# A chunked RWKV-7 recurrence on one core: outputs with both heads of a pair side by side, turned by four full transposes a chunk; keys turned by eight

## The chip, the cores and the metric

The kernel is one launch on one core of a Trainium2 chip. The core has five engines with a queue each, which run their instructions in order: TensorE (PE in the rows; its weight loads are PEld), VectorE (DVE), ScalarE (ACT), GpSimd (POOL) and SyncE (SP), which issues the DMAs. The metric is the device time of the launch in microseconds (us); the number compared is the median of several runs.

## The reference, cut to what matters

The program is one step of a two-layer encoder over 1024 prompt tokens and 64 sample tokens, with 1024 features in 16 heads of 64. Layer 0 mixes time by a recurrence per head over the tokens, and then has a feed-forward part; layer 1 has windowed attention and a second feed-forward part. The change is in the recurrence:

```
def step(s, inp):                       # s [head, value, key]
    r_t, w_t, k_t, v_t, a_t, b_t = inp
    sa = einsum('bhvk,bhk->bhv', s, a_t)
    s = s * w_t[:, :, None, :] + sa[..., None] * b_t[:, :, None, :] + v_t[..., None] * k_t[:, :, None, :]
    return s, einsum('bhvk,bhk->bhv', s, r_t)
...
s_fin, y = lax.scan(step, s0, seq_in)
yc = y - mean(y, axis=-1, keepdims=True)
yn = yc * rsqrt(mean(yc * yc, axis=-1, keepdims=True) + LNX_EPS)
yn = yn.reshape(bsz, t_len, D_MODEL) * lnx_w + lnx_b
bonus = (sum(rh * kh * r_k, axis=-1, keepdims=True) * vh).reshape(bsz, t_len, D_MODEL)
out = ((yn + bonus) * g) @ w_o
```

## The kernel before

Two kinds of work share the core. The dense products (projections, feed-forward, lines 422 to 424) take each fp32 operand as two float32r parts and sum three matmuls; their weights come by DMA, are cast on ACT (L382) and subtracted on DVE or POOL (L383). The recurrence (class `Rwkv`, tiles named `r_...`, its PSUM tiles `p_rp`, `p_rc`, `p_ry`) works in 17 chunks of 64 tokens: eight, then eight, then the sample's one. All of its products go through `mm` (L73) and `tr` (L77), so that tiles, not lines, tell them apart.

A chunk has four parts. `prep` makes the scaled keys `BK`, queries `AR` and the triangles `X` (tile `r_G`), which need no state. `prep2` inverts the triangles, mostly on DVE, and turns the keys into `BT`. `chain` is what the state `M` passes through: `U0p`, `Up`, the state's increment `Sp`, and the outputs `Y` (tile `p_ry`, one buffer), which are the sum of `AR` times the state and `X` times the stacked operand `sv`. `post` normalises `Y` over the 64 values of each head on DVE, ACT and POOL into `yc`, turns `yc` back to features on the partitions in the place of `Y`, applies the gate `g` and writes `z`.

The heads stand in pairs: head 2j on partitions 0 to 63, head 2j + 1 on 64 to 127. In `Y` of before, the partition is (head of the pair, token) and the free axis (pair, value). A full transpose of a pair's columns would mix both heads, so `post` turns each head by itself:

```
for j in range(8):
    self.tr(Y[0:64, j, :], yc[0:64, j, :], c["id"][0:64, 0:64])
    self.mm(Y[64:128, j, :], lhsT=yc[64:128, j, :], rhs=c["id"][64:128, 64:128], start=True, stop=True)
```

The order on each engine is fixed when the program is built: a scheduler emits the instruction of the lowest priority number that it holds to be ready. `recur` gives the chain and `prep2` a number ahead of the dense work, and `prep` and `post` of a chunk one behind it for all but their products, so that dense products fill PE between the recurrence's pieces. At run time the queues are fixed, and an instruction that waits holds up what stands behind it on its engine.

Of the kernel before, what the change touches and what calls it, by code (L numbers as in the profile page):

```python
# [21 lines left out]
def bc(ap, n):  # L22
    """[p, a] -> [p, a, n], each value n times"""
    return ap.unsqueeze(len(ap.shape)).broadcast_to(list(ap.shape) + [n])


def mid(ap, n):
    """[p, a] -> [p, n, a], the row n times"""
    return ap.unsqueeze(1).broadcast_to([ap.shape[0], n] + list(ap.shape[1:]))


class Two:
    """Puts the products of a stream of instructions at another priority than the rest of it."""
# [15 lines left out]
class Rwkv:  # L49
    """The chunked WKV-7 recurrence: chunks of 64 tokens, 16 heads in 8 pairs."""  # L50
# [20 lines left out]
    def mm(self, *a, **k):  # L71
        with self.two:
            self.nc.tensor.matmul(*a, **k)  # L73
# [8 lines left out]
    def start(self):  # L82
        """the part of W that stays zero"""
        nc = self.nc
        self.W = self.sb.tile([128, 8, 64], F32, name="W", tag="W", bufs=1)
        nc.gpsimd.memset(self.W, 0.0)

    def prep(self, ch):
        """all that does not need the state; heads 2j on partitions 0-63, heads 2j + 1 on 64-127"""
# [13 lines left out]
        # 1 / |kk|^2 as the lanes of inverse() hold it: [(parity, half of the tokens, 4 times, pair), token]  # L103
# [12 lines left out]
        # the products of the decays up to each token, and before it  # L116
# [10 lines left out]
        # r P  # L127
        V.tensor_tensor(out=AR[:, :, 1, :], in0=r, in1=P, op=ALU.mult)
        # k (1 + (a - 1) k_a)
# [4 lines left out]
        # kk a / P and -kk Pex without the norm of kk, whose square inverse() divides by  # L134
# [3 lines left out]
        # r k r_k  # L138
# [3 lines left out]
        # the four triangles of each head: [(b, k) of the key, (a, r) of the query]  # L142
# [10 lines left out]
        # sum(r k r_k) v  # L153
# [7 lines left out]
    def prep2(self, d):  # L161
# [4 lines left out]
        # the strict triangle of b is spent: a takes its place  # L166
# [3 lines left out]
        flat2 = lambda x: x.rearrange("p a b -> p (a b)")  # L170
        BT = d["BT"] = self.t([128, 16, 64], "BT")
        ps = [self.pp().rearrange("p (a b) -> p a b", a=8) for _ in range(2)]
        for i in range(8):
            for par in range(2):
                h = slice(64 * par, 64 * par + 64)
                self.tr(ps[par][:, i, :], flat2(d["BK"][h, i]), self.c["id"][h, h])
        for par in range(2):
            S.copy(BT[:, 8 * par:8 * par + 8, :], ps[par])

    def inverse(self, X, nl):  # L180
        """D (I - T D)^-1 of the strict triangles T, transposed, with D = 1 / |kk|^2: first the blocks of 32 by
        substitution, a lane for each block and each fourth of its rows, then the block beside them"""
        nc, c = self.nc, self.c
        V, S, G = nc.vector, nc.scalar, nc.gpsimd
        W = self.W
# [13 lines left out]
        # two columns j, j + 1 at a time: row j + 1 takes what it adds by way of column j  # L199
        one = NL.rearrange("p a b -> p (a b)")[:, 32:1024:66]  # L200
        ev = NL.rearrange("p (a two) b -> p a two b", two=2)
        # Z: rows 8 r + 4 h + (0 .. 3) in the half h, so that neither half waits for what it has just written
# [7 lines left out]
        for j in range(30, 0, -2):  # L210
            # from the first place to the last, and back
# [19 lines left out]
        for h in range(2):  # L231
            XO = Z[:, h, 1].rearrange("p a b -> p (a b)")                   # [s, (r g pair)]
            V.transpose(out=XO, in_=XL[:, h].rearrange("p a b -> p (a b)"))
# [24 lines left out]
    def chain(self, ch, d, M):  # L258
        """M [128 = (parity, key), pair, value]: the state's transpose; returns the next"""
        nc = self.nc  # L260
        V, S, G = nc.vector, nc.scalar, nc.gpsimd
        # rows of the stacked operands: the state, later U, on 0-63; the values on 64-127
# [11 lines left out]
        for i, j, h in heads:  # L274
            self.mm(Y[h, j, :], lhsT=d["AR"][h, j, 1, :], rhs=M[h, j, :], start=j == 0, stop=False)
# [8 lines left out]
        for i, j, h in heads:  # L284
            self.mm(Sp[h, j, :], lhsT=BT[:, 8 * (i % 2) + j, :], rhs=sv[:, i, :], start=True, stop=True)
        for i, j, h in heads:
            self.mm(Y[h, j, :], lhsT=X[:, 8 * (i % 2) + j, 64:128], rhs=sv[:, i, :], start=False, stop=j == 7)
# [5 lines left out]
    def post(self, ch, d, Y):  # L293
# [18 lines left out]
        # back to the features on the partitions, in the place of Y  # L312
        for j in range(8):
            self.tr(Y[0:64, j, :], yc[0:64, j, :], c["id"][0:64, 0:64])
            self.mm(Y[64:128, j, :], lhsT=yc[64:128, j, :], rhs=c["id"][64:128, 64:128], start=True, stop=True)
# [9 lines left out]
TA, TB, TBJ = 512, 576, 580          # tokens of the halves; TBJ: with the columns between the streams  # L325
SOFF = 516                           # first column of the sample stream in a TBJ wide tile
SCALE = 0.125

# columns of `vecs`: [128, 8] each, feature = 128 * column + partition
# [4 lines left out]
RING, EXTRA, EARLY = 11, 4, 13       # pairs of operand tiles; more after the recurrence, and before it  # L334
# [5 lines left out]
class Dense:  # L340
    """Products with the features on the partitions: both operands cut into two float32r parts."""
# [12 lines left out]
    def st(self, w=584):  # L354
        return self.t([128, w], "st", 4)

    def tmp(self):
        """like st(), with tiles of its own as long as there are the early ones"""
        return self.t([128, 580], "es", 4, sb=self.esb) if self.esb else self.st()
# [11 lines left out]
    def weight(self, src, rows=128, raw=None):  # L371
        """a [rows, n] block of DRAM in pieces of 512 columns, each as (hi, lo)"""
# [14 lines left out]
    def part(w, o, n):  # L387
        """columns of a weight"""
# [4 lines left out]
    def pair(self, late=False):  # L393
        """the two tiles of an operand; late: it outlives the early ones"""
# [4 lines left out]
    def free(self, *pairs):  # L399
        """the last instruction that reads them is out"""  # L400
# [6 lines left out]
    def split(self, x, rows=128, eng=None, late=False):  # L407
        """x as a pair"""
# [9 lines left out]
    def mm(self, ps, parts):  # L418
        """ps = sum of the products; parts: (w hi, w lo, x hi, x lo)"""
# [6 lines left out]
    def full(self, src, xs, groups, evac):  # L426
        """one tile of 128 outputs of a product over 8 x 128 features"""
# [6 lines left out]
    def first(self, ws, xs, groups, evac):  # L434
        """full() of three tiles of outputs, which take each operand in turn as it comes"""
# [11 lines left out]
    def low(self, src, M, tag):  # L447
        """the weights of a low-rank product, as long as there are the early tiles: for each tile of features
        the high parts of its M columns, and beside them the low ones"""
# [10 lines left out]
    def low_banks(self, tag, groups):  # L460
        """banks of the recurrence, before it starts"""
# [3 lines left out]
    def low_step(self, ps, w, k, x, groups):  # L465
        """what the tile k of the features adds; up to 64 columns take the high part of x with both of theirs"""
# [10 lines left out]
    def low_sum(self, p, M, n):  # L477
        """of the products with the two parts of the weights"""
# [5 lines left out]
    def behind(self, i, before):  # L484
        """i waits for an instruction that it does not depend on"""
# [3 lines left out]
    def stack(self, t, x, q):  # L489
        """x [n, .] into the columns q of t [2 n, .]: its two parts, one below the other"""  # L490
# [5 lines left out]
class Norm:  # L496
    """1 / rms of each token, on all partitions, from tiles that come one by one"""
# [17 lines left out]
    def finish(self):  # L515
        """in two steps, for other products to come between them"""
# [11 lines left out]
        # diagonal blocks, which a product with ones spreads over the partitions  # L528
# [13 lines left out]
def go(job, *sides):  # L542
    """emits a job, with a step of each of the sides after each of its own"""
# [8 lines left out]
def several(n, gen):  # L552
    """n steps of a generator in one"""
# [8 lines left out]
def tile_stream_step(ctx: ExitStack, tc: tile.TileContext, I, O):  # L562
# [13 lines left out]
    def load(half):  # L576
        """the input; the column before the tokens is left for the row before them"""
# [17 lines left out]
    # the table of Sqrt, before it is waited for  # L595
# [9 lines left out]
    # 1 - mu  # L605
# [9 lines left out]
    def put(name, half, j, stg):  # L615
        """the feature tile j of a half into the chunks of a scratch array"""
# [6 lines left out]
    def inputs(half, hs):  # L623
        """the normalised input with the row before it in column 0"""
# [16 lines left out]
        for j, h in enumerate(hs):  # L641
            if j in pool:
                G.tensor_tensor(out=h[:, 1:T + 1], in0=h[:, 1:T + 1], in1=rs[:, :T], op=ALU.mult)
            else:
                i = V.scalar_tensor_tensor(out=h[:, 1:T + 1], in0=h[:, 1:T + 1], scalar=vec["norm_mix0"][:, j:j + 1], in1=rs[:, :T],
                                           op0=ALU.mult, op1=ALU.mult)
                # not ahead of the first products' operands
# [26 lines left out]
    def streamed(hs, half, name, step):  # L674
        """mixes whose tiles are spent one step after they come"""
# [5 lines left out]
    def decay(half, hs):  # L681
# [10 lines left out]
        # the rows of ones take w0, whose parts are on the rows 64 and 96  # L692
# [3 lines left out]
        def summed(hh, ch, n, sg):  # L696
            """over the tokens of each chunk"""
# [33 lines left out]
    def rate(half, hs, two):  # L731
        """two: a pair, its first tile for this, the second for gate()"""
# [64 lines left out]
    def rkv(half, name, xs, ws=()):  # L797
        """ws: the weights of the first tiles of outputs, which are there already"""
# [3 lines left out]
        def tokens(j, stg):  # L802
            """the values with the tokens on the partitions"""
# [50 lines left out]
    def held(gen):  # L854
        """the tiles of a mix, each once a pair that lasts is free for it"""
# [14 lines left out]
    def mixed_in(half, get, xs, res):  # L870
        """the outputs of the recurrence, which pass through the places of the residual stream"""
# [10 lines left out]
    def mix_out(half, xs, norm):  # L882
        """w_o of the time mixing, and the residual stream"""
# [9 lines left out]
    def fresh(half, x, fast=False):  # L893
        """the next norm of a residual stream"""
# [4 lines left out]
    def normed(norm, gain, xs):  # L899
        """the residual stream, normalised with a gain"""  # L900
# [11 lines left out]
    class Ffn:  # L912
        """keep: of how many pairs of tiles the second product is left to rest()"""
# [107 lines left out]
    def recur(chunks, M, base, low):  # L1021
        """the chunks in turn, what does not need the state one chunk ahead"""
# [104 lines left out]
class Attention:  # L1127
    """Grouped-query attention over the band of three chunks, with sinks. The tile m * 4 + i of the queries
# [284 lines left out]
```

## Time and profile before

| what | value |
|---|---|
| median of 3 runs | 3094.4 us (3092.99 to 3098.16) |
| the profiled execution, first to last instruction | 3098.9 us |
| PE busy | 2948.1 us, 95% |
| DVE busy | 1905.6 us, 61% |
| ACT busy | 1371.1 us, 44% |
| POOL busy | 921.6 us, 30% |
| recurrence on PE | from about 260 to 1215 us |

The page gives one execution. Of what lies around the span the page has no figure; the span is 4.5 us above the median of the runs. Busy shares are means over the whole span, in which the recurrence takes less than a third.

### The profile page before, as it was taken

How to read it: one execution, taken by the hardware profiler on the slowest of the kernel's cores; microseconds unless marked ns; L12 is line 12 of the kernel's file. 1: busy time of each engine (PE TensorE's matmuls, PEld its weight loads, DVE VectorE, ACT ScalarE, POOL GpSimd, SP SyncE). 2: the span in 40 equal slices, each digit the busy share in tenths (PEclk: the TensorE clock that was granted, in tenths of full speed). 3: DMA queues.
4: the chain of work that ended last, by engine and by line, in shares of the span. 5: the costliest groups of instructions: out<-in, count | busy, mean ns of one | idle time of the engine just before them, and what ended most of it. 6: DMA issues, size and time to landing. Idle time of an engine off the chain costs nothing. (4 is left out here: it accounts for less than half of the span.)

```text
span 3098.9 us, 52449 instructions
## 1 busy us (share of the span) xinstructions
PE 2948.1 (95%) x20126; PEld 2520.6 (81%) x20126; DVE 1905.6 (61%) x3964; ACT 1371.1 (44%) x2489; POOL 921.6 (30%) x768
## 2 busy tenths in 40 slices
PE   6899898998899999999999999999999999999998
PEld 5677677886677777887778999888667889899998
DVE  8887788968898984356654333565555334633334
ACT  6767655434555442344553222344454233322222
POOL 6464233423333322224311222243111222322221
PEclk9998778988899999999999999999999999999999
DMA  4645443334223224332212222222122332322222
GB/s 143 171 121 152 116 123 91 106 99 143 79 83 96 86 66 127 103 112 84 70 45 69 82 82 82 76 84 82 55 65 65 96 96 75 102 83 83 85 85 69
DMA packets 262051, 289.16 MB, mean 93 GB/s; under 512 B 125028, under 2 KB 143972, under 8 KB 261800
## 3 DMA queue, kind: packets, MB, share of 16 engines
q1 hardware_dynamic: 261800, 285.81, 30.8%
q8 instruction: 158, 2.59, 0.3%
q14 instruction: 93, 0.76, 0.1%
HBM read 243.18 MB, written 41.16 MB: 92 GB/s over the span
## 5 line engine op out<-in xcount | busy, mean ns | idle before, releaser
L422 PE MATMUL dp<-xh,wh 128*128 128x288 f32 (+2 forms) x3480 | 1184.5, 342 | 26.5 <-DVE hx L951 7.0
L423 PE MATMUL dp<-xl,wh 128*128 128x288 f32 (+2 forms) x3480 | 1174.9, 338 | 9.5 <-DVE xl L415 6.9
L424 PE MATMUL dp<-xh,wl 128*128 128x288 f32 (+2 forms) x3480 | 1172.3, 337 | 0.0
L382 ACT CAST wh<-wr 128x512 fp32r<-128x512 f32 x730 | 445.8, 619 | 821.7 <-PE dp L423 635.2
L422 PEld LDWEIGHTS dp<-xh,wh 128*128 128x128 f32 x3480 | 669.2, 193 | 100.5 <-DVE hx L951 9.9
L423 PEld LDWEIGHTS dp<-xl,wh 128*128 128x128 f32 x3480 | 669.9, 193 | 72.3 <-DVE xl L415 8.8
L424 PEld LDWEIGHTS dp<-xh,wl 128*128 128x128 f32 x3480 | 670.2, 193 | 61.4 <-issue 5.6
L383 DVE TENSOR_TENSOR wl<-wr,wh 128x512 fp32r<-128x512 f32 x487 | 377.6, 779 | 444.2 <-ACT wh L382 435.5
L383 POOL TENSOR_TENSOR wl<-wr,wh 128x512 fp32r<-128x512 f32 x243 | 336.0, 1383 | 997.3 <-ACT wh L382 894.1
L422 PE MATMUL dp<-mh,wh 128*128 128x288 f32 (+1 forms) x808 | 255.0, 316 | 3.6 <-DVE hx L951 2.6
L424 PE MATMUL dp<-mh,wl 128*128 128x288 f32 (+1 forms) x808 | 254.6, 315 | 0.0
L423 PE MATMUL dp<-ml,wh 128*128 128x288 f32 (+1 forms) x808 | 253.8, 314 | 0.0
L951 DVE TENSOR_TENSOR a_xB<-dp,a_xB 128x288 f32<-128x288 f32 x352 | 158.1, 456 | 82.4 <-PE dp L424 81.9
L932 DVE TENSOR_TENSOR st<-st,dp 128x288 f32<-128x288 f32 (+1 forms) x132 | 70.0, 531 | 216.8 <-PE dp L424 216.4
L934 POOL TENSOR_TENSOR xl<-st,xh 128x288 fp32r<-128x288 f32 (+1 forms) x102 | 101.2, 993 | 334.2 <-ACT xh L933 322.1
L422 PEld LDWEIGHTS dp<-mh,wh 128*128 128x128 f32 x808 | 152.5, 189 | 13.5 <-DVE hx L951 3.8
L424 PEld LDWEIGHTS dp<-mh,wl 128*128 128x128 f32 x808 | 152.4, 189 | 8.1 <-issue 1.8
L423 PEld LDWEIGHTS dp<-ml,wh 128*128 128x128 f32 x808 | 152.6, 189 | 6.8 <-issue 0.8
L951 DVE TENSOR_TENSOR hx<-dp,hx 128x512 f32<-128x512 f32 x176 | 119.8, 685 | 48.2 <-PE dp L424 47.9
L191 ACT COPY r_f<-r_G 32x1024 f32<-32x1024 f32 x68 | 134.7, 1981 | 32.5 <-DVE r_G L152 21.2
L216 DVE TENSOR_TENSOR r_f<-r_f,r_f 128x60 f32<-128x60 f32 (+5 forms) x476 | 117.5, 278 | 0.5
L930 ACT ACTIVATE st<-dp 128x288 f32<-128x288 f32 (+1 forms) x132 | 62.2, 471 | 93.2 <-PE dp L424 92.8
(344 smaller groups left out, 4003.3 us busy)
## 6 DMA issues: line engine op xcount, KB each, us to landing
wr<-in_ffn_in SPq DMA_DIRECT2D x352, 256.0 KB
wr<-in_ffn_out SPq DMA_DIRECT2D x176, 256.0 KB
wr<-in_rkv SPq DMA_DIRECT2D x90, 256.0 KB
wr<-in_rwo SPq DMA_DIRECT2D x32, 256.0 KB
wr<-in_wq SPq DMA_DIRECT2D x32, 256.0 KB
wr<-in_wo SPq DMA_DIRECT2D x32, 256.0 KB
r_r_s<-s_s SPq DMA_DIRECT2D x17, 256.0 KB
r_sv<-s_vt SPq DMA_DIRECT2D x17, 256.0 KB
```

The source lines that it names most:

```text
L191: S.copy(st[32 * q:32 * q + 32].rearrange("p (t g j) -> p t g j", g=4, j=8), src)
L216: V.tensor_tensor(out=Z[:, h, 1:3, r0:4, 0:j], in0=Z[:, h, a, r0:4, j:j + 2].rearrange("p r c -> p c r").unsqueeze(3).broadcast_to([128, 2 ...
L382: nc.scalar.copy(h, x)
L383: (nc.gpsimd if self.turn % 3 == 0 else nc.vector).tensor_tensor(out=l, in0=x, in1=h, op=ALU.subtract)
L422: self.nc.tensor.matmul(ps, lhsT=wh, rhs=xh, start=i == 0, stop=False)
L423: self.nc.tensor.matmul(ps, lhsT=wh, rhs=xl, start=False, stop=False)
L424: self.nc.tensor.matmul(ps, lhsT=wl, rhs=xh, start=False, stop=i == last)
L930: S.activation(t[o], p, AF.Silu)
L932: V.tensor_tensor(out=t[o], in0=t[o], in1=p, op=ALU.mult)
L934: G.tensor_tensor(out=a.lo[:, q], in0=t[o], in1=a.hi[:, q], op=ALU.subtract)
L951: V.tensor_tensor(out=self.x[m][:, q], in0=p, in1=self.x[m][:, q], op=ALU.add)
```

## The change

Three things change. The remaining lines of the diff remove comments and docstrings, so that later line numbers move by up to 11.

1. `Y` gets another layout: the partition is (parity of the pair's number, token), and the free axis (pair of pairs, head of the pair, value), so both heads of a pair stand side by side in 128 columns. `post` then turns `yc` by four transposes of 128 x 128 in place of eight transposes and eight products of 64 x 64.
2. The part of `Y` from the state was 16 products in a row, of the two heads of each pair in turn. Now the eight even heads come first (`seen(0)`), the eight odd heads after (`seen(1)`). Both groups write the same partitions from different rows of the array, and between them stands a one-element memset on POOL, `by`, which waits for the last even product and for which the first odd one waits. The products with `X` go through the pairs in another order.
3. The keys are turned by eight transposes of 128 x 128 in place of sixteen of 64 x 128, and `BT` is indexed by head.

```
     def mm(self, *a, **k):
         with self.two:
-            self.nc.tensor.matmul(*a, **k)
+            return self.nc.tensor.matmul(*a, **k)
...
         BT = d["BT"] = self.t([128, 16, 64], "BT")
-        ps = [self.pp().rearrange("p (a b) -> p a b", a=8) for _ in range(2)]
-        for i in range(8):
-            for par in range(2):
-                h = slice(64 * par, 64 * par + 64)
-                self.tr(ps[par][:, i, :], flat2(d["BK"][h, i]), self.c["id"][h, h])
-        for par in range(2):
-            S.copy(BT[:, 8 * par:8 * par + 8, :], ps[par])
+        for g in range(2):
+            ps = self.pp()
+            for i in range(4):
+                self.tr(ps[:, 128 * i:128 * i + 128], flat2(d["BK"][:, 4 * g + i]), self.c["id"])
+            S.copy(flat2(BT[:, 8 * g:8 * g + 8, :]), ps)
...
-        for i, j, h in heads:
-            self.mm(Y[h, j, :], lhsT=d["AR"][h, j, 1, :], rhs=M[h, j, :], start=j == 0, stop=False)
+        out = lambda j, par: Y[64 * (j % 2):64 * (j % 2) + 64, j // 2 * 2 + par, :]
+
+        def seen(par):
+            h = slice(64 * par, 64 * par + 64)
+            return [self.mm(out(j, par), lhsT=d["AR"][h, j, 1, :], rhs=M[h, j, :], start=par == 0 and j < 2, stop=False) for j in range(8)]
+        even = seen(0)
+        by = G.memset(self.t([1, 1], "by", 2), 0.0)
...
         for i, j, h in heads:
-            self.mm(Sp[h, j, :], lhsT=BT[:, 8 * (i % 2) + j, :], rhs=sv[:, i, :], start=True, stop=True)
-        for i, j, h in heads:
-            self.mm(Y[h, j, :], lhsT=X[:, 8 * (i % 2) + j, 64:128], rhs=sv[:, i, :], start=False, stop=j == 7)
+            self.mm(Sp[h, j, :], lhsT=BT[:, i, :], rhs=sv[:, i, :], start=True, stop=True)
+
+        odd = seen(1)
+        for i, first in ((by, even[-1]), (odd[0], by)):
+            info = mybir.DependencyInfo(mybir.DependencyClass.Sync, mybir.DependencyReason.DATA)
+            self.tc.add_manual_dep(i.ins, first.ins.name, info, reason="rows")
+        for q in range(0, 8, 2):
+            for j, par in ((q, 0), (q + 1, 0), (q, 1), (q + 1, 1)):
+                self.mm(out(j, par), lhsT=X[:, 8 * par + j, 64:128], rhs=sv[:, 2 * j + par, :], start=False, stop=q == 6 and par == 1)
...
-        for j in range(8):
-            self.tr(Y[0:64, j, :], yc[0:64, j, :], c["id"][0:64, 0:64])
-            self.mm(Y[64:128, j, :], lhsT=yc[64:128, j, :], rhs=c["id"][64:128, 64:128], start=True, stop=True)
+
+        for q in range(0, 8, 2):
+            self.tr(flat(Y[:, q:q + 2, :]), flat(yc[:, q:q + 2, :]), c["id"])
```

On PE, in the ninth chunk, the turn of `yc` stood like this before (the pair of rows comes eight times; `dp` is a dense product's bank, `p_rp` the turned keys):

```order
L422 MATMUL dp_11344<-xh_11182,wh_11332 128x512
L423 MATMUL dp_11344<-xl_11183,wh_11332 128x512
L77 MATMUL p_ry_7897<-c_id,r_yc_7996 64x64 [waits DVE_49,Pool_49]
L73 MATMUL p_ry_7897<-c_id,r_yc_7996 64x64
...
L77 MATMUL p_rp_8500<-c_id,r_BK_8204 128x64 [waits DVE_49]
L77 MATMUL p_rp_8501<-c_id,r_BK_8204 128x64 [waits DVE_49]
```

The same place of the changed program:

```order
L434 MATMUL dp_10999<-xl_10901,wh_10993 128x512
L435 MATMUL dp_10999<-xh_10900,wl_10994 128x512
L77 MATMUL p_ry_7745<-c_id,r_yc_7846 128x128 [waits Pool_49]
L77 MATMUL p_ry_7745<-c_id,r_yc_7846 128x128 x3
L433 MATMUL dp_11038<-xh_10858,wh_11026 128x512 [waits Activation_49]
...
L77 MATMUL p_rp_8320<-c_id,r_BK_8034 128x128 [waits DVE_49]
L77 MATMUL p_rp_8320<-c_id,r_BK_8034 128x128 x3
```

Sixteen instructions of two kinds became four of one kind, and sixteen turned keys two groups of four.

On PE, three chunks later, the products with the state were one group of sixteen among dense products:

```order
L424 MATMUL dp_11805<-xh_11194,wl_11800 128x512
L422 MATMUL dp_11805<-xh_11200,wh_11799 128x512
L73 MATMUL p_ry_8953<-r_M_8689,r_AR_8555 64x64 [waits DVE_49]
L73 MATMUL p_ry_8953<-r_M_8689,r_AR_8555 64x64 x15
L73 MATMUL p_rc_8830<-r_ixd_8801 32x32 [waits Activation_49]
L423 MATMUL dp_11805<-xl_11201,wh_11799 128x512
```

In the changed program they are two groups of eight:

```order
L73 MATMUL p_ry_8747<-r_M_8503,r_AR_8367 64x64 [waits DVE_49]
L73 MATMUL p_ry_8747<-r_M_8503,r_AR_8367 64x64 x7
L77 MATMUL p_rp_8988<-c_id,r_BK_8702 128x128
...
L433 MATMUL dp_11461<-xh_11066,wh_11441 128x512 [waits DVE_49]
...
L435 MATMUL dp_11461<-xh_11235,wl_11448 128x512
L73 MATMUL p_ry_8747<-r_M_8503,r_AR_8367 64x64 [waits Pool_49]
L73 MATMUL p_ry_8747<-r_M_8503,r_AR_8367 64x64 x7
L433 MATMUL dp_11469<-xh_11066,wh_11441 128x512 [waits DVE_49]
```

Five turned keys and six dense products stand between the groups here; the second group now waits for POOL, and dense products stand behind it.

On POOL, in the chunk before that one, before the change (`r_vf<-r_vf,r_g` is the gate times the bonus of the recurrence, `wl` the low part of a weight):

```order
L299 TENSOR_TENSOR r_vf_8592<-r_vf_8592,vecs 128x512 [waits DMAHW2_49,DVE_49]
L300 TENSOR_TENSOR r_vf_8240<-r_vf_8240,r_g_8692 128x512 [waits DMAHW6_49]
L383 TENSOR_TENSOR wl_11710<-wr_11711,wh_11709 128x512 [waits DMAHW3_49,PE_49,Activation_49]
L301 TENSOR_TENSOR r_g_8692<-r_g_8692,vecs 128x512 [waits Pool_49]
L101 TENSOR_TENSOR r_rt_9232<-r_r_k_9225,vecs 128x8x64 [waits DMAHW1_49]
```

The same place of the changed program:

```order
L311 TENSOR_TENSOR r_vf_8404<-r_vf_8404,vecs 128x512 [waits DMAHW2_49,DVE_49]
L312 TENSOR_TENSOR r_vf_8070<-r_vf_8070,r_g_8506 128x512 [waits DMAHW5_49]
L281 MEMSET r_by_8439 1x1 [waits PE_49]
L313 TENSOR_TENSOR r_g_8506<-r_g_8506,vecs 128x512 [waits Pool_49]
L101 TENSOR_TENSOR r_rt_9008<-r_r_k_9001,vecs 128x8x64 [waits DMAHW7_49]
```

The memset `r_by` is new on POOL and stands here behind an instruction that waits for a DMA; in twelve of the seventeen chunks the instruction just ahead of it waits for a DMA, for ACT or for DVE.

## Rows read from the trace of the kernel before

**Rows 1.** The page: busy us, share of the span, instructions by engine.

```profile
PE 2948.1 (95%) x20126; PEld 2520.6 (81%) x20126; DVE 1905.6 (61%) x3964; ACT 1371.1 (44%) x2489; POOL 921.6 (30%) x768
```

**Rows 2.** Busy us (x instructions) by stretch of the recurrence, then clock, DMA share, GB/s.

```profile
400.00:540.00 140.00, 124.23 (x1162) 106.92 (x1163) 117.71 (x298) 83.10 (x131) 48.29 (x34) 0.80 0.39 105
540.00:700.00 160.00, 152.79 (x1692) 135.03 (x1690) 124.91 (x337) 71.32 (x118) 57.77 (x42) 0.88 0.38 105
...
760.00:900.00 140.00, 127.60 (x1051) 98.29 (x1051) 124.87 (x287) 76.87 (x104) 53.59 (x39) 0.88 0.26 82
900.00:1050.00 150.00, 142.34 (x1213) 108.92 (x1212) 133.89 (x353) 76.54 (x101) 55.16 (x43) 0.93 0.30 94
1050.00:1220.00 170.00, 167.36 (x1473) 130.09 (x1473) 129.47 (x349) 66.91 (x99) 47.28 (x37) 0.92 0.25 77
```

**Rows 3.** Timeline of PE, first and last of 17 turns of yc (start us, us).

```profile
378.80 0.30 PE L77 MATMUL p_ry<-c_id,r_yc 64*64 64x64 f32 x1
...
383.91 0.61 PE L751 MATMUL dp<-xh,wh 128*128 128x290 f32 x1
...
1211.21 0.24 PE L77 MATMUL p_ry<-c_id,r_yc 64*64 64x64 f32 x1
1211.38 0.32 PE L73 MATMUL p_ry<-c_id,r_yc 64*64 64x64 f32 x2
...
1214.38 0.47 PE L73 MATMUL p_ry<-c_id,r_yc 64*64 64x64 f32 x2
1214.78 0.79 PE L424 MATMUL dp<-xh,wl 128*128 128x512 f32 x1
```

**Rows 4.** Timeline of PE at full transposes elsewhere in the kernel (start us, us).

```profile
265.56 0.60 PE L806 MATMUL dp<-c_id,st 128*128 128x128 f32 x4
265.99 0.27 PE L813 MATMUL dp<-c_id,st 128*64 128x128 f32 x1
...
2074.37 1.12 PE L1182 MATMUL dp<-c_id,st 128*128 128x128 f32 x4 [5.45 <-ACT st L1202]
2075.28 0.42 PE L1186 MATMUL dp<-c_id,st 128*64 128x128 f32 x1
```

**Rows 5.** Stretches from a turn of yc on, columns as in rows 2.

```profile
532.00:545.00 13.00, 13.00 (x127) 9.89 (x126) 8.22 (x14) 11.26 (x11) 3.54 (x2) 0.74 0.26 77
576.00:590.00 14.00, 14.00 (x98) 11.00 (x97) 13.93 (x22) 13.47 (x17) 4.42 (x4) 0.62 0.21 58
...
1211.00:1224.00 13.00, 13.00 (x60) 9.93 (x59) 4.06 (x6) 1.86 (x3) 3.16 (x3) 0.87 0.43 120
```

**Rows 6.** One turn of yc, what follows, and attention with full transposes, as rows 2.

```profile
1211.00:1214.00 3.00, 3.00 (x22) 1.92 (x20) 0.00 (x0) 0.00 (x0) 0.00 (x0) 1.00 0.30 93
1214.20:1217.60 3.40, 3.40 (x12) 2.62 (x11) 1.38 (x2) 0.62 (x1) 0.39 (x1) 0.52 0.11 42
...
2150.00:2400.00 250.00, 250.00 (x1120) 172.63 (x1119) 133.96 (x306) 120.01 (x300) 41.94 (x46) 1.00 0.20 62
```

**Rows 7.** Timeline of PE: turned keys of one row half, then a chunk's products.

```profile
288.00 0.71 PE L77 MATMUL p_rp<-c_id,r_BK 64*128 64x64 f32 x8
...
1093.55 1.15 PE L73 MATMUL p_ry<-r_M,r_AR 64*64 64x64 f32 x32
...
1094.80 1.15 PE L73 MATMUL p_rc<-r_sv,r_G 128*64 128x64 f32 x32
...
1096.50 0.71 PE L77 MATMUL p_rp<-c_id,r_BK 64*128 64x64 f32 x16
```

**Rows 8.** Waits (us in total, times, longest): PE from 540 to 760, POOL from 250 to 1220.

```profile
PE p_ry L77 <- POOL r_yc L311: 5.5, 1, 5.5
...
POOL wl L383 <- ACT wh L382: 152.0, 30, 12.3
...
POOL r_vf L300 <- DMA r_g<-s_g: 43.4, 9, 10.3
```

**Rows 9.** Who waited for the tile p_ry (us, times).

```profile
  DVE r_g L316: 23.5, 9
```

## The prediction

> **What bounds the kernel now.** The page first: PE is busy for 2948.1 of 3098.9 us, and no other engine for more than two thirds [rows 1]. But the change touches only the recurrence, so the second view is busy time by stretch [rows 2]. There PE shares the load: it has 95% from 540 to 700 us and 98% from 1050 to 1220 us, and in these stretches a microsecond taken off PE is one off the time, because dense products stand ready in its queue. From 400 to 540 and from 760 to 1050 us DVE has 84% to 89% and PE 89% to 95%, and what PE saves may turn into waiting for DVE. The reader is also to see the clock in these rows: 0.80 to 0.93 of full speed, where PE lives in two levels, 2.4 and 1.2 GHz.
>
> The third view is the timeline of PE at the pieces that change. A turn of yc takes 3.57 us at the full clock, 1211.21 to 1214.78, and 5.11 us at the half, 378.80 to 383.91 [rows 3]. That is long for its size: 32 fp32 passes of 64 columns elsewhere in the chunk take 1.15 us [rows 7], these 24 take three times as long, a pair of one transpose and one product every 0.43 us. The pairs are not overlapped with each other, as the products of rows 7 are. I read the same two times, start to the next group's start, in all 17 chunks: 3.43 to 5.12 us each, 67.0 us together.
>
> The fourth view is the clock behind a turn. In the last chunk it is 1.00 during the turn and 0.52 in the 3.4 us behind it [rows 6], where dense products run at half their rate. From single-microsecond windows I find the full clock before and such a fall 3 to 6 us after the start in 11 of the 17 chunks. Windows of 13 or 14 us from the start show 0.62 in one, 0.74 in six and 0.87 in four of them [rows 5]; one less the clock, times the length, is 5.3 + 6 x 3.4 + 4 x 1.7 = 32.5 us of PE's time at full speed.
>
> **The change, part by part.**
>
> *The turn of yc.* Sixteen instructions (24 records) go, four full transposes come. Four of that form take 0.60 us from the first start to the last end at full clock and 1.12 at half, with the next group begun 0.43 and 0.91 us after the first [rows 4]. I take 0.65 for a mean chunk: 67.0 - 17 x 0.65 = 56 us of PE. This is the surest term; its bounds are 17 x 0.43 and 17 x 1.12, so 48 to 60.
>
> *The clock behind it.* The block that stands ahead of each fall shrinks to a sixth, and attention, where full transposes stand between other products, ran from 2150 to 2400 us at 1.00 [rows 6]. But other small products of the recurrence stand near each turn, and they remain. I take two thirds of 32.5 back, 22 us; bounds 0 and 32.
>
> *The keys.* Sixteen transposes of one row half each take 0.71 us when both halves follow each other, and eight of one half alone take 0.71 as well [rows 7], so a chunk costs 0.71 or 1.42. Eight full ones are two groups of rows 4, 1.03 to 1.2 us at full clock. Per chunk that is between 0.5 dearer and 0.4 cheaper; I take nothing, with +8 and -7 us as bounds. What would hide it is the dense work of the same queue, and in the PE-bound stretches nothing does.
>
> *The state's products in two groups.* Sixteen products (32 records) in 1.15 us become two groups of eight that use the same 64 rows and in turn two column halves. The nearest row for column halves alone is the product of sv and the triangles, whose 32 records of 128 x 64 take the same 1.15 us [rows 7]: column halves overlap as well as diagonal pairs do. Then only a second fill is added, about 0.2 us a chunk, 3 us. If two tiles on the same rows don't overlap, the group doubles, as the lone half of the keys does: 1.1 us a chunk, 18 us. I take 3, as the row nearest in form.
>
> *The detour over POOL.* In the order the second group stands behind 8 to 52 other instructions of PE, most of them dense products. The memset waits for PE, then the odd products for the memset; whatever stands behind them on PE, all of it dense work or the next pieces of the chain, waits too. What the memset costs is a wait in POOL's queue: POOL stood 43.4 us in 9 waits for the gate's DMA and 152.0 us in 30 waits for ACT's casts [rows 8], about 5 us each, and the memset often stands right behind one of these. Against that, PE waited on POOL for yc, which stands in the same queue, once for 5.5 us, between 540 and 760 us [rows 8], and in no other of the 17 chunks. I take one such wait in the whole recurrence, 6 us; bounds 0 and 43, as much as the DMA waits hold in all. VectorE, ScalarE and SyncE get the same number of instructions.
>
> *The sum.* 56 + 22 + 0 - 3 - 6 = 69 us off PE's queue.
>
> *What of it reaches the end.* Of the 17 turns, eight lie in the two stretches of rows 2 where PE has 95% and more, and count in full. The other nine (378 to 533 and 823 to 1023 us) lie where PE also waits and DVE has up to 89%; I count half. 69 x (8 + 4.5) / 17 = 51 us. Something speaks for more: DVE waited for the turn 23.5 us in nine chunks before it could apply the gate [rows 9], and these waits shrink with it. Next in line where PE is lighter is DVE, with its inversion of the triangles. Behind 1220 us nothing changes but that less dense work is left.
>
> Against the profiled execution that is 3098.9 - 51 = 3048 us. It lies 4.5 us above the median, and I carry the difference: 3094.4 - 51 = 3043.5, so **3044 us**.
>
> *A rule to weigh.* One transposition of rows 4 lasts 0.27 us by itself, but the next starts 0.11 us after it. The Trainium skill, TensorE: Matmul & The Clock Gate, Part 4 (PE-mode transpose), gives about 275 ns for one 128 x 128 transpose in a kernel. Worked out from that page as an estimate, twelve of them would be 3.3 us a chunk, 56 us in all, where the sum above has 17 x (0.65 + 1.1) = 30. The rows bear out its duration of one, not that one behind another costs as much.
>
> **The rivals.**
>
> *VectorE takes over* (0.15). If the recurrence in all stretches is held by DVE, what PE saves becomes idle time, and only DVE's own waits for the turn come back: 3094 - 23 = 3071 us. For it: 89% of DVE from 760 to 1050 us. Against it: 76% to 78% of DVE where PE is full [rows 2].
>
> *All of it arrives* (0.10). The clock no longer falls behind the turns, and dense work fills everything: 56 + 32 - 3 = 85, 3010 us.
>
> *Each transpose costs its whole duration* (0.04). At 0.27 us [rows 4] the 12 take 3.2 us a chunk, 55 in all, against 67.0 and about 17 x 1.0 before: 29 us saved, and with the other terms (29 + 22 - 9) x 12.5 / 17 = 31, 3063 us. The spacing of rows 4 is against it. This is what the page's rule named above comes to.
>
> *POOL holds PE* (0.06), the case on the other side. If the memset in every chunk stands behind a wait of the kind in rows 8, about 5.1 us, PE loses 17 x 5.1 = 87 us and gains 75: 3106 us. It decides from 75 / 17 = 4.4 us a chunk. For it: twelve of 17 memsets stand behind an instruction that waits for a DMA, ACT or DVE. Against it: POOL is busy for less than a third of its time, and its one wait above.
>
> *Nothing is left* (0.07). The whole order of the recurrence was made anew by the scheduler, so that weights and loads move against each other on all queues; single waits of several microseconds on PE come and go by that, and could eat a gain of the clockless kind, 3094.
>
> **How the numbers follow.** The forecast, a gain of 25 to 75 us, has 0.58; its own range is 3019 to 3069. A measurement can tell about 0.2%, 6 us, from no change. Faster: 0.58 + 0.15 + 0.10 + 0.04 = 0.87; same 0.07; slower 0.06. The range takes in full arrival at 3010 and the VectorE case with a few microseconds for the detour, 3078; it leaves out the last two rivals and the edges.
>
> **What would show it.** The turn of yc as four records in 0.4 to 0.6 us at full clock, and no fall of the clock behind most of them: a granted clock above that of rows 2 in each stretch. PE busy some 60 to 70 us shorter over the whole span, at a similar busy share in the recurrence. The odd group with a wait for POOL in at most a few chunks. The recurrence's last turn nearer 1170 than 1211 us. I am wrong if PE's waits for DVE and ACT from 250 to 1220 us grow by what it saves, if the two groups of state products take over 2 us together, or if PE waits for `by` in most chunks.

## The result, and the profile after

The changed kernel takes 3068.4 us (median of 4 runs, 3065.7 to 3072.4) against 3096.3 for the kernel before: a ratio of 0.9911, interval 0.9897 to 0.9925. That is a gain of 28 us, on the forecast side, but little more than half of the 51 that were forecast; 3068.4 lies less than a microsecond inside the range of 3019 to 3069. Two single executions, 3537 us in run 4 and 10696 us in the kernel before with vf first, stand far from all others of their kernels and count in no time below.

The page's line of busy time, to be held against [rows 1]:

```profile
span 3066.4 us, 51529 instructions
PE 2881.6 (94%) x19650; PEld 2475.1 (81%) x19650; DVE 1899.9 (62%) x3964; ACT 1371.4 (45%) x2489; POOL 915.9 (30%) x785
```

PE is busy 66.5 us less (2948.1 to 2881.6), and the span is 32.5 us shorter. The rest is waiting: span less PE's busy time was 150.8 us and is 184.8. So PE's queue lost most of what was forecast (69, or 75 without the wait for POOL), and 34 us of it came back as idle time.

The turn of yc, last of 17, on PE's timeline (start us, us), against [rows 3]:

```profile
1189.94 0.39 PE L435 MATMUL dp<-xh,wl 128*128 128x512 f32 x1
1190.17 0.60 PE L77 MATMUL p_ry<-c_id,r_yc 128*128 128x128 f32 x4
1190.53 0.48 PE L433 MATMUL dp<-xh,wh 128*128 128x512 f32 x1
1190.84 0.39 PE L434 MATMUL dp<-xl,wh 128*128 128x512 f32 x1
```

0.36 us from the first transpose to the next product, in place of 3.57, and the dense products behind it keep a spacing of 0.23 to 0.31 us, the full clock. The same in windows from a turn on (columns as in rows 2), against [rows 5]:

```profile
1190.00:1203.00 13.00, 13.00 (x60) 10.51 (x59) 8.87 (x14) 2.88 (x5) 3.17 (x3) 1.00 0.73 180
1105.00:1118.00 13.00, 12.98 (x118) 9.80 (x116) 10.03 (x33) 8.51 (x6) 3.55 (x4) 1.00 0.27 81
```

The clock stays at 1.00. Within 6 us of the start it falls anew behind two of the 17 turns, in the second and third chunk, where it did behind 11; two more turns begin at half the clock already. In the kernel before PE was busy for the whole of every microsecond from the turn's start to the fall, in all 11 cases; the two falls that are left come behind microseconds in which PE stands idle or nearly so (from 422 us on in the one, 465 to 467 in the other). From 200 to 1250 us, one less the clock summed over single microseconds was 124.6 us and is 100.7.

The stretches of [rows 2] after the change:

```profile
400.00:540.00 140.00, 118.08 (x1230) 105.05 (x1230) 122.85 (x305) 86.89 (x139) 50.30 (x43) 0.87 0.44 118
540.00:700.00 160.00, 140.30 (x1506) 124.90 (x1504) 126.39 (x344) 81.60 (x125) 54.87 (x45) 0.89 0.44 117
...
760.00:900.00 140.00, 127.74 (x1042) 99.79 (x1037) 127.55 (x327) 71.84 (x101) 49.78 (x40) 0.88 0.26 80
900.00:1050.00 150.00, 138.03 (x1185) 107.17 (x1183) 138.61 (x360) 74.98 (x101) 52.94 (x42) 0.94 0.31 96
1050.00:1220.00 170.00, 160.31 (x1278) 126.20 (x1278) 118.09 (x288) 68.11 (x100) 52.66 (x43) 0.94 0.34 99
```

The reader is to look at PE in the second and the last row. From 540 to 700 us it was idle for 7.2 us and is for 19.7, from 1050 to 1220 for 2.6 and now 9.7. These are the stretches that I had called full (a stretch is one of time; the recurrence in it is now up to 28 us further on). DVE is up by a few microseconds in the first four rows: the recurrence goes faster (its last turn stands at 1190 us, not 1211).

What PE waits for now, from 250 to 1220 us (us in total, times, longest):

```profile
PE p_rc L73 <- ACT r_ixd L246: 15.2, 7, 4.3
PE p_rp L73 <- ACT r_rt L102: 10.0, 2, 8.8
PE dp L711 <- ACT st L733: 8.8, 2, 6.8
PE p_rc L73 <- DVE r_ixd L236: 7.9, 4, 3.4
...
PE p_rc L73 <- DVE r_ixd L247: 5.9, 3, 3.0
...
PE p_ry L73 <- POOL r_by L281: 3.2, 3, 1.5
```

The same view of the kernel before:

```profile
PE p_rc L73 <- DVE r_ixd L237: 6.5, 3, 3.0
...
PE p_rc L73 <- ACT r_ixd L247: 4.7, 1, 4.7
```

The tile r_ixd belongs to the inversion of the triangles: DVE makes it, PE multiplies, ACT and DVE copy it, PE multiplies again. PE waited 13.2 us for these three steps (2.0 of it for the copy on DVE, not shown) and now waits 29.0. All its waits for DVE and ACT in this window together went from 64.5 to 95.6 us, which is 31 more. The detour over POOL is the last row: 3.2 us of PE's own waiting.

### The profile page after: what moved, and what is told of

It is laid out like the page before. It is cut to its first block, busy times and chain, and to the rows that moved or that the text cites. A ratio compares the mean times of both kernels' runs of the same rounds, so it can differ in the third digit from the quotient of the medians.

```text
span 3066.4 us, 51529 instructions
## 1 busy us (share of the span) xinstructions
PE 2881.6 (94%) x19650; PEld 2475.1 (81%) x19650; DVE 1899.9 (62%) x3964; ACT 1371.4 (45%) x2489; POOL 915.9 (30%) x785
## 5 line engine op out<-in xcount | busy, mean ns | idle before, releaser
L944 ACT CAST xh<-st 128x288 fp32r<-128x288 f32 (+1 forms) x102 | 50.2, 492 | 136.2 <-DVE st L943 135.1
```

The lines of the kernel that those rows point to most:

```text
L944: S.copy(a.hi[:, q], t[o])
```

## Experiments

Differences between kernels of one work but another order turned out to matter, so each run is also read by two numbers from its profile: PE's busy time, and the span less that.

**1. The keys alone.**

```
-        for i in range(8):
-            for par in range(2):
-                h = slice(64 * par, 64 * par + 64)
-                self.tr(ps[par][:, i, :], flat2(d["BK"][h, i]), self.c["id"][h, h])
...
+            for i in range(4):
+                self.tr(ps[:, 128 * i:128 * i + 128], flat2(d["BK"][:, 4 * g + i]), self.c["id"])
...
```

> Of the change this takes only the eight full transposes of the keys; the outputs stay as before. Theory (the turn of yc and the clock behind it made the gain): no difference that can be told, 3094 to 3099 us, since eight full transposes take PE about as long as sixteen halves. Rival (the keys carry a good part of the 28 us): 3085 us or less. A second rival (any edit of the recurrence gives the scheduler another order, worth 10 us either way): more than 6 us off in either direction.

Measured: 3104.2 us, ratio 1.0039 (1.0024 to 1.0053), so 12 us slower than the kernel before in the same runs. The page's lines:

```profile
span 3101.5 us, 52224 instructions
PE 2936.8 (95%) x19990; PEld 2519.3 (81%) x19990; DVE 1898.8 (61%) x3964; ACT 1374.6 (44%) x2490; POOL 926.3 (30%) x768
```

PE is busy 11 us less, and idle 164.7 us, 14 more. My expectation of no difference failed; the second rival, that any edit gives another order, fits.

**2. The outputs alone.** The new layout, the two groups and the four transposes, with the keys as before.

```
...
-            S.copy(flat2(BT[:, 8 * g:8 * g + 8, :]), ps)
...
+            S.copy(BT[:, 8 * par:8 * par + 8, :], ps[par])
...
```

> The new layout of the outputs, the two groups of state products with the memset on POOL, and the four full transposes of yc, with the keys turned as before. Theory: nearly all of the gain, 3065 to 3073 us, and the clock falls behind at most two turns. Rival (the keys): 3080 us or more.

Measured: 3087.8 us, ratio 0.9988 (0.9976 to 1.0000): 4 us faster. Of the 14 turns that begin at the full clock none is followed by a fall within 6 us; of the other three two are, once the clock has risen, and there PE stands idle for a microsecond or two just before.

```profile
span 3090.0 us, 51802 instructions
PE 2890.1 (94%) x19786; PEld 2484.8 (80%) x19786; DVE 1902.0 (62%) x3964; ACT 1371.5 (44%) x2491; POOL 918.9 (30%) x785
```

The busy time fell by 58 us, as it should; the idle time rose by 49, to 199.9. The times of the parts don't add up: 12 us slower and 4 faster apart, 28 faster together. PE's busy time does, 11 and 58 us less apart and 66.5 together; its waiting does not, 14 and 49 more apart and 34 together. The expectation that the outputs alone bring nearly all of the gain failed on that. The rival's number came (3080 us or more) but not its reason: the keys alone made the kernel slower.

**3. The two groups in the kernel before**, with the old layout and the old turn.

```
+        seen = lambda par: [self.mm(Y[h, j, :], lhsT=d["AR"][h, j, 1, :], rhs=M[h, j, :], start=j == 0, stop=False) for i, j, h in heads[par::2]]
+        even = seen(0)
+        by = G.memset(self.t([1, 1], "by", 2), 0.0)
...
```

> The kernel before, with its old layout and old turn, but with the state's products in two groups of eight and the memset on POOL between them. Theory (the detour is cheap, PE waits for the memset a few times for under 2 us): 3096 to 3106 us, at most 10 above before. Rival (the detour takes back the 20 us that the forecast had too much): 3115 us or more, with PE waiting for the memset in most chunks.

Measured: 3124.8 us, ratio 1.0095 (1.0079 to 1.0112), 33 us slower than before: the rival's number. But it is not the detour. Groups by line, with what ended the idle time before them:

```profile
L73 PE MATMUL p_ry<-r_M,r_AR 64*64 64x64 f32 x544 | 45.0, 241 | 2.7 <-DVE r_AR L128 1.7 <-POOL r_by L276 0.7 <-DVE r_g L321 0.2
```

and the same groups in the kernel before and in the changed one:

```profile
L73 PE MATMUL p_ry<-r_M,r_AR 64*64 64x64 f32 x544 | 23.6, 248 | 1.8 <-DVE r_AR L128 1.7
```

```profile
L73 PE MATMUL p_ry<-r_M,r_AR 64*64 64x64 f32 x544 | 26.7, 240 | 9.0 <-DVE r_g L327 4.0 <-POOL r_by L281 3.2 <-DVE r_AR L128 1.7
```

PE waited for the memset for 0.7 us. What grew is the products themselves: in the old layout a group of eight even heads lies on one quarter of the array, and eight in a row on one quarter take 45.0 us where pairs on two quarters take 23.6. In the changed kernel a group goes in turn to two column halves, and takes 26.7. Those 21 us are not all of the 33. PE's busy time rose by 28 in the profile and its idle time fell by 12; the mean granted clock of the runs was 0.948, against 0.956 for the kernel before in the same runs, and no run shows why. The experiment did not isolate the detour, as I meant it to, but it prices both bounds of the forecast's term: 3 us as taken, 21 for the case without overlap (18 was forecast).

**4. A long turn of full transposes.** The changed kernel with its four transposes made seven times; the output is the same.

```
-        for q in range(0, 8, 2):
+        for q in 7 * [0, 2, 4, 6]:
             self.tr(flat(Y[:, q:q + 2, :]), flat(yc[:, q:q + 2, :]), c["id"])
```

> The changed kernel with its four transposes of yc made seven times over, 28 in place of 4, so that the turn takes PE about 3.1 us again, near the 3.6 of before, but in full transposes. The output is the same. If PE's time is what binds the stretch, 17 x 2.6 = 44 us more PE work costs 30 us or more, 3098 us or above. If, as I now think, about half of what PE saves became waiting, the added work fills some of these waits: 3080 to 3095 us. If the clock falls behind long turns whatever they are made of, 8 or more of the 17 turns show a fall again; if it was the mixed small products, at most 3 do.

Measured: 3115.9 us, ratio 1.0081 (1.0065 to 1.0096). The page's line, PE's timeline, and windows from three turns on:

```profile
PE 2922.4 (94%) x20058; PEld 2521.4 (81%) x20058; DVE 1904.1 (61%) x3964; ACT 1376.7 (44%) x2494; POOL 929.3 (30%) x785
```

```profile
1214.99 0.40 PE L435 MATMUL dp<-xh,wl 128*128 128x512 f32 x1
1215.23 3.22 PE L77 MATMUL p_ry<-c_id,r_yc 128*128 128x128 f32 x28
1218.20 0.48 PE L433 MATMUL dp<-xh,wh 128*128 128x512 f32 x1
```

```profile
533.00:546.00 13.00, 12.12 (x154) 10.85 (x154) 9.10 (x12) 10.63 (x11) 5.33 (x5) 1.00 0.31 83
877.00:890.00 13.00, 13.00 (x91) 10.39 (x91) 13.00 (x39) 1.24 (x2) 5.15 (x5) 1.00 0.32 96
1215.00:1228.00 13.00, 13.00 (x72) 11.08 (x71) 3.37 (x5) 3.13 (x6) 3.08 (x3) 1.00 0.53 142
```

The turn takes 2.97 us, near the 3.57 of before, and within 6 us of the start the clock falls behind none of the 17 turns (two begin at half the clock already). In three chunks it falls 7 to 10 us after the start, each time behind one or more microseconds in which PE stands idle. So the falls of the kernel before did not come from the turn's length, but from what it was made of; whether the mixture of kinds or the small tiles count, no run separates. The second finding goes against my theory of slack: PE's busy time rose by 41 us, from 2881.6 to 2922.4, and the waits did not shrink to make room for it (188.6 against 184.8 us idle). The time rose by 47. But DVE's gate waits for the turn, so this run delays DVE as well as it loads PE, and does not show that PE's time alone binds.

**5 and 6, 7 and 8. The same work in another order**, twice, in the kernel before and in the changed one. First the loads of a chunk:

```
-        for x, n in ((s, "s"), (k, "k"), (a, "a"), (r, "r")):
+        for x, n in ((k, "k"), (s, "s"), (r, "r"), (a, "a")):
```

> The kernel before, with nothing changed but the order in which a chunk's four loads are issued (k, s, r, a in place of s, k, a, r), which gives the scheduler another order on every engine with the same work. Theory (what PE saves turns in part into waits, whatever the order): within 12 us of before, and PE idle from 200 to 1250 us between 60 and 90 us. Rival (the order made by the scheduler decides as much as the change): more than 12 us from before, or idle time above 95 us.

> The changed kernel with the same swap of loads. Theory: 20 to 36 us below the kernel before with the same swap, PE idle from 200 to 1250 us between 100 and 125 us, PE busy 60 to 70 us less over the span. Rival (order decides): a gain under 15 or over 45 us against its partner, with the same saving of PE's busy time.

then the load of vf moved ahead of them:

```
+        vf = self.t([128, 8, 64], "vf", 3)
+        nc.sync.dma_start(flat(vf), self.scr["v"][ch])
         kkr, sq = self.tmp(), self.tmp()
```

> The kernel before, with the load of the values vf issued ahead of a chunk's other loads: again the same work in another order. Theory: within 12 us of before, idle time of PE from 200 to 1250 us between 60 and 90 us. Rival: further off.

> The changed kernel with vf loaded first. Theory: 20 to 36 us below its partner, idle time of PE between 100 and 125 us. Rival: a gain under 15 or over 45 us.

Measured, the ratios of the last two pairs against the kernel before in the same runs (3095.5 us), and read from the page's span and PE's busy time; idle is the one less the other:

| pair | before | changed | gain | PE busy saved | idle grown |
|---|---|---|---|---|---|
| as given | 3096.3 | 3068.4 | 28 | 66.5 | 34.0 |
| loads k, s, r, a | 3111.1 (1.0053, 1.0040 to 1.0065) | 3058.7 (0.9880, 0.9866 to 0.9893) | 52 | 71.4 | 20.0 |
| vf first | 3091.9 (0.9988, 0.9978 to 0.9998) | 3067.2 (0.9909, 0.9896 to 0.9923) | 25 | 47.4 | 25.3 |

From 200 to 1250 us PE was idle for 82 and 81 us in the two of before, 102 and 108 in the two of the changed kernel; before as given had 74, the changed kernel 108. Within a column the order alone is worth up to 19 us. With the loads swapped both expectations of the time failed: the kernel before was 16 us off, and the gain of the changed one over 45 us, which was the rival's; with vf first both held. The idle times held in all four. Across the rows the sign is the same three times: PE's work falls by 47 to 71 us, its waiting grows by 20 to 34. Of 185 us saved in the three together 79 came back as waits, so 57% arrived.

Two things go with the spread; neither is shown to be its cause. The mean granted clock of the runs rose from 0.956 (43 executions) to 0.959 as given, from 0.951 to 0.962 with the loads swapped and from 0.957 to 0.959 with vf first, so the largest gain has the largest rise. (The profile of the kernel before with vf first shows 0.960, as much as that of its partner; PE's busy time in it is 20 us below that of before as given, with the same work.) And PE's waits for r_ixd, 13.2 and 29.0 us as given, are 29.9 and 32.4 with the loads swapped, 14.3 and 31.1 with vf first: near 30 us in all three changed kernels, but in one kernel before as well, by its order alone.

The swap of loads with the change is also the fastest kernel that I ran.

**9 and 10. A load on VectorE.** Five products more in each chunk's preparation, whose result nothing reads.

```
+        for _ in range(5):
+            V.tensor_tensor(out=self.t([128, 7, 64], "spare"), in0=AR[:, 0:7, 1, :], in1=r[:, 0:7, :], op=ALU.mult)
```

> The kernel before with five products of 128 x 448 more on VectorE in each chunk's preparation, whose result nothing reads: about 3 us a chunk, 51 us of VectorE in all; no PE work is added. Theory (VectorE and what hangs on it hold the recurrence already in part of the stretch, and more so after the change): 10 to 30 us above before. Rival (PE alone binds before, the waits after the change are single accidents of order): within 10 us of before.

> The changed kernel with the same load on VectorE. Theory: it costs here more than in the kernel before, by 10 us or more, since PE now reaches its waits earlier: 3095 to 3115 us, PE idle from 200 to 1250 us 130 us or more. Rival: the same cost as in the kernel before, or less.

Measured: 3115.7 us (1.0068, 1.0051 to 1.0085) with the load in the kernel before, 21 us above it; 3120.6 (1.0093, 1.0074 to 1.0112) in the changed kernel, 52 above its 3068.4. From 250 to 1250 us, before and changed without the load:

```profile
250.00:1250.00 1000.00, 928.27 (x8068) 755.14 (x8067) 799.89 (x2042) 506.60 (x756) 328.96 (x249) 0.88 0.36 105
```

```profile
250.00:1250.00 1000.00, 894.41 (x7734) 736.90 (x7733) 808.60 (x2061) 517.78 (x775) 333.80 (x273) 0.90 0.38 109
```

and with it:

```profile
250.00:1250.00 1000.00, 904.88 (x7983) 740.25 (x7982) 841.05 (x2118) 501.73 (x750) 328.24 (x247) 0.87 0.35 103
```

```profile
250.00:1250.00 1000.00, 847.85 (x7515) 703.36 (x7514) 851.56 (x2121) 504.71 (x752) 334.66 (x263) 0.87 0.36 103
```

DVE's busy time there is 841 and 852 us, 41 and 43 above the kernels without the load. The same load costs half its length in the kernel before and more than its whole length in the changed one, where it takes back all of the gain: with the load the changed kernel is 5 us slower than the kernel before with it, and the clock is the same in both (0.951 and 0.952 in the mean of the runs). The time expected for the changed kernel (3095 to 3115 us) was passed by 6 us; that the load costs more here, and 130 us or more of idle time from 200 to 1250 us (it is 154), came true. PE's longest waits in the loaded changed kernel:

```profile
PE p_rc L73 <- DVE r_ixd L238: 25.4, 7, 8.9
PE p_rc L73 <- ACT r_ixd L248: 18.9, 7, 6.9
```

They are those that had grown with the change, for the inversion. The order is new here too, and one order moved a kernel by up to 19 us above, so some of the 31 us between the two costs may be chance.

**11 and 12. VectorE lightened**: every second weight's low part on POOL, in place of every third, in the two kernels with the loads in the order k, s, r, a.

```
-        (nc.gpsimd if self.turn % 3 == 0 else nc.vector).tensor_tensor(out=l, in0=x, in1=h, op=ALU.subtract)
+        (nc.gpsimd if self.turn % 2 == 0 else nc.vector).tensor_tensor(out=l, in0=x, in1=h, op=ALU.subtract)
```

> The kernel before with the loads in the order k, s, r, a, and with every second weight's low part made on POOL in place of every third, which takes a sixth of these subtractions off VectorE. Theory: no gain or a small one against the same kernel without it, 3100 to 3115 us. Rival (VectorE binds before as well): under 3095 us.

> The changed kernel with the loads in the order k, s, r, a, and every second low part on POOL. Theory (VectorE takes part of what PE saves): 3040 to 3055 us, 5 to 20 below the same kernel without it. Rival (POOL's slower subtraction holds the dense work): 3060 us or more.

Measured: 3108.5 us (1.0050, 1.0035 to 1.0065) in the kernel before with swapped loads, 3 below the one without it; 3079.7 (0.9959, 0.9943 to 0.9976) in the changed one, 21 above. So this pair's gain is 29 us, where it was 52 without the edit. The expectation for the kernel before held, that for the changed kernel failed: its rival's number, 3060 us or more, came. It does not show DVE to be free: the longest wait of PE there is again for DVE's part of the inversion.

```profile
PE p_rc L73 <- DVE r_ixd L236: 27.4, 10, 6.0
```

Whether POOL's slower subtraction or the new order did it stays open.

## Why the prediction was right, and where its size was off

*The turn of yc* (56 us): right. From the first start to the next group's start, 67.0 us in 17 chunks became 12.3, so 55.

*The clock behind it* (22 us): right in the profiled pair, 124.6 to 100.7 us, and the cause is shown further than the forecast had it: no fall within 6 us behind 28 full transposes of nearly the same length (run 4). But part of that size is luck. The profile of before has a mean granted clock of 0.952, the lowest that 43 other executions of the same kernel had (0.952 to 0.960). One less the clock, times the span, is 148.7 us in it and 122.7 in the profile of the changed kernel, 26 less; as the mean of those 43 executions and of the changed kernel's four it is 136.6 and 126.5, only 10 less.

*The keys* (nothing): right for PE, whose time for them went from 20.7 to 21.7 us by the groups.

*The state's products* (3 us): right, 23.6 to 26.7 us; the bound of 18 is what a group on one quarter costs (21, run 3).

*The detour over POOL* (6 us): right. PE's products waited 3.2 us, three times; with the weight loads in front of them, which PE's queue holds too, the tile's view has 8.4 us in eight waits. The rival that POOL holds PE did not come; in the other orders of the changed kernel PE's products waited 10.3 us (loads k, s, r, a) and 4.1 (vf first).

*The sum*: 69 forecast, of which the 6 for POOL are waiting and not work, so 75 off PE's busy time; 66.5 measured. The terms as measured (55 and 24, less 1 and 3) come to 75 as well; where the other 8 us went is open.

*What of it reaches the end* is the term that was mis-sized: 51 of 69 forecast, 32.5 of 66.5 in the profile. I had counted the eight turns from 540 to 700 and from 1050 to 1220 us in full, "because dense products stand ready in its queue". The rows after show that the idle time grew most just there, by 12.5 and 7.1 us. That PE is 95% busy said what bound it with the old turn in the queue, not how far ahead the next engine was. PE now waits longer at the inversion's products for what DVE and ACT make, 29.0 us in place of 13.2, and since its queue is in order, the dense products behind stand too. That it is the saving which brings PE there too early is argued and not shown apart from the order: the kernel before with the loads swapped waits 29.9 us there. The forecast named this as the rival *VectorE takes over*, at 3071 us, and the measured time is 3 us from that and 24 from the forecast, so that it lies in the forecast's range is in part luck; the text beside the chances names another range, 3010 to 3078. But the rival's reason was only partly right. It had DVE's waits for the turn as all that comes back (they fell from 23.5 us in nine chunks to 5.4 in three); what binds in the changed kernel is not DVE alone. A longer turn on PE (run 4) and a load on DVE (run 10) both cost their length or more.

Of the signs named, the turn in four records came, and the clock rose in four of the five stretches of rows 2 and stayed at 0.88 in the fifth. The last turn, at 1190 us, is midway between the 1170 expected and 1211. The first sign of being wrong came by half: PE's waits for DVE and ACT grew by 31 us, of 66.5 saved.

The rival *each transpose costs its whole duration* fell: 28 stand in 2.97 us, 0.106 us apart. The rival *nothing is left* was near for parts of the change: its reason, that the scheduler makes a new order, is what runs 1 and 2 and the three pairs show, with up to 19 us for the same work.

What stays open: how the 28 us of the given pair split between the change and its order. Three pairs give 25 to 52, mean 35. Two of the waits that grew most, for r_rt (10.0 us, two times) and st (8.8 us, two times), are a few long events, which depend on the order more than on the change: both stand with the same length in the changed kernel with vf first, and are 2.8 and 5.7 us in the one with the loads swapped, while the kernel before with the loads swapped has 8.1 us for r_rt.

## What to carry to other kernels

Take a saving on a busy engine in two steps: what leaves its queue can be read from rows to within a few microseconds, while what reaches the end depends on how soon the next engine is waited for, and a stretch at 95% can hide a second engine that is just behind. With a scheduler's order, compare the same work in two or three orders before an edit of half a per cent is believed, on either side. Where a block of small products takes several times its passes, look for a mixture of kinds in it, and at the clock in the microseconds behind it. The clock differs between executions of one kernel too, so a term read from one profile is to be held against the clocks of all runs.

## What the runs showed of the hardware that was not expected

Transposes of 64 x 64 alternated with fp32 products of another quarter took 0.43 us a pair at the full clock, and within 6 us of the start of 11 of 17 such blocks the granted clock fell to the 1.2 GHz level, though the profile shows PE busy throughout; 28 full transposes back to back, 0.106 us each and 2.97 us together at the full clock, had no fall within 6 us of the start in any of the 17 chunks. The Trainium skill, TensorE: Matmul & The Clock Gate, Part 4 (PE-mode transpose), gives about 275 ns for a transpose in a kernel: the duration of one agrees (272 ns), the spacing is less than half of it. Eight fp32 products in a row on one quarter of the array take nearly twice what they take in turn on two quarters, be these on the diagonal or side by side on the same rows (45.0, 23.6 and 26.7 us for the 272 products of 17 chunks).
